# A fused decoder layer: one accumulator per PSUM bank in the first feed-forward product, copies and stores moved from the first to the second block, and a scheduler's cost table rewritten

## The chip, the cores and the metric

The kernel runs on one core of one Trainium2 chip. The metric is the device time of one execution in microseconds (us). Three runs of the kernel before gave 2949.49, 2956.81 and 2946.39 us, median 2949.49. The core's engines each work through a queue of their own in order: PE (TensorE, matrix products into PSUM), DVE (VectorE) and ACT (ScalarE, both elementwise work, both able to read PSUM), POOL (GpSimd) and SP (SyncE, which here only issues the DMAs).

## The reference

One decoder layer on 2048 tokens of width 1024, in fp32. Cut to what matters:

```
proj = x @ w_in                               # q, k, v, z, gates, memory queries
o = gated_delta_rule(conv(q, k, v), gates)    # 8 heads of 128, chunked, a state carried along
m = memory_attention(mq, mem_k, mem_v)        # 4 heads over 256 memory rows
x = layer_norm(ALPHA * x + concat(o, m) @ w_out)
x = layer_norm(ALPHA * x + square(relu(x @ w_ff1)) @ w_ff2)   # width 1024 -> 4096 -> 1024
```

## The kernel before

**Blocks and stages.** The tokens go through in four blocks of 512 (`for b in range(NB)`, near the end of `hybrid_layer`). Each block has a stage with the heads (here MIX: projections, delta rule and memory attention), the output projection (OUT, `out_proj`, with the first layer norm in `norm1`), and the feed-forward part, `ff_seven` (line 1169). That one runs over four groups g of 1024 hidden features. For each group it makes the hidden activations (here FF1) and then their product with `w_ff2` (FF2).

**Precision.** Every fp32 operand is split in two: `hi` is the value rounded to the PE's fp32r (a copy on ACT), `lo` is the remainder (a subtraction on DVE). A product is three matmuls: hi hi, hi lo, lo hi. So a 128x1024 weight tile costs a load, one ACT cast and one DVE subtraction before PE can use it. A tile that was split once can be kept in DRAM as a pair: `keep_hilo` (line 494) stores it, `load_hilo` (line 498) loads both halves with no work on ACT or DVE. `hilo_in` (line 486) loads an fp32 tile and splits it using two of the weight buffers; `hilo(load_raw(...))` (lines 475 and 480) takes three. There are `NW = 11` weight buffers.

**Seven products.** FF2 in all blocks, and FF1 in blocks 1 to 3, use a Winograd form with seven products in place of eight for a 2x2 partition of the operands. The sums of weight parts (`S1`-`S4` of `w_ff1`, `T`-like sums of `w_ff2`) are made in block 0 and kept in DRAM (`fsc`, `tsc`). In FF1 of blocks 1 to 3 the token side is split into `B11, B21, B22, T1-T4` by `to_quads` (line 641) after the layer norm, token groups in the order 2, 3, 0, 1. There a unit v is 256 features; a group has two, so a block has eight. `ff1_quads` (line 1416) runs the seven products of a unit in the order of `FF1_SEVEN` (line 1136). A product is 24 matmuls of 128x256, 12 for each half i of the unit. The accumulators, named A, B and C:

- A gathers A11, S2, S1 and S4 in turn, and is read on the way after each of them. C gathers S3 and A22, and is read after each. B holds A12.
- A and C of one half lie in one PSUM bank, A in the first 256 columns and C in the second. Both halves of B lie in another bank. `read` (line 1444) takes each part out with an ACT copy or a DVE addition, adds the parts up, applies relu and square, and splits the result as input of FF2.
- For the first group both units run interleaved: their A11 and A12 come first, since these need only token groups 2 and 3.

PSUM has eight banks, under five tags: `acc` 3, `ga0`, `ga1` and `m` one each, `pb` 2.

**DRAM traffic around it.** In block 0, FF1 is a plain product. It stores the split parts of every `w_ff1` tile for later (`keep_parts`, line 1144, into `fhl`), and block 0's head iterations issue DRAM-to-DRAM copies of three parts of `w_ff2` (`copy_rows`, line 1114, into `fcp`), which FF2 loads in every block. `load_out` (line 537) splits `w_out` in block 0, stores the pairs (`osc`) and loads them in blocks 1 to 3.

**What sets the order.** Nothing runs when it is written. `Recorder` (line 140) records every operation; `issue` (line 230) then simulates the five engines with a table of durations (`cost`, line 192), latencies between engines (`LAT`, `LAT_FROM`), buffers and one DMA pipe. Each engine takes, of what is ready in that model, the operation with the lowest index (`nc.shift` adds to the index). The resulting order per engine is fixed in the program; at run time semaphores make each engine wait for what it needs.

Of the kernel before, what the change touches and what calls it, by code (L numbers as in the profile page):

```python
# [139 lines left out]
class Recorder:  # L140
# [51 lines left out]
    def cost(o, name, wr, rd, args, kw):  # L192
# [15 lines left out]
        if e == "SP":  # L208
            o.extra = 2100 + _prod(wr[0].shape if wr else rd[0].shape) * 4 / 390.0
            return 450  # L210
        scal = [v for v in args[2:] if isinstance(v, Ref)] if name.startswith("tensor_scalar") else []
        scal += [v for k, v in kw.items() if k in ("scalar", "scalar1", "scale", "bias") and not isinstance(v, (int, float))]
        if e == "ACT":
            n = _prod((wr[0]).shape[1:])
            return 52 + 0.833 * n + (0 if psum else 42) + 93 * len(scal) + ((305 if scal else 198) if "accum_out" in kw else 0)
        if e == "DVE":
            fast = not psum and name in ("tensor_copy", "tensor_scalar_mul", "tensor_scalar_add", "tensor_scalar_max",
                                         "memset")
            return 68 + (0.52 if fast else 1.042) * n + 62 * len(scal) + (7 * n if name == "reciprocal" else 0)
        if name == "memset":  # L220
            return 40 + 0.83 * n
        if kw.get("op") == ALU.pow:
            return 840 + 38 * n
        if name == "tensor_copy":
            return 150 + 1.3 * n
        if name == "tensor_tensor":
            return 150 + 3.5 * n
        return 134 + 3.14 * n if n > 8 else 500 if n == 1 else 200

    def issue(self):  # L230
# [50 lines left out]
        while True:  # L281
# [70 lines left out]
def hybrid_layer(  # L352
# [184 lines left out]
    def load_out(b, u, nh):  # L537
        if b == 0:
            hi, lo = hilo(load_raw(w_out[u, nh]))
            keep_hilo(osc[u, nh], hi, lo)  # L540
        else:
            hi, lo = load_hilo(osc[u, nh])
# [98 lines left out]
    def to_quads(y, Q, keep, t):  # L641
# [11 lines left out]
        if t < 2:  # L653
            nc.shift = 200 if t == 0 else 130
# [12 lines left out]
            quad_split(Q, "T2", t, s["T2"])  # L667
            quad_split(Q, "T3", t, s["T3"])
            quad_split(Q, "B22", t, b22)
            quad_split(Q, "T1", t, s["T1"])  # L670
            quad_split(Q, "T4", t, s["T4"])
# [389 lines left out]
    def mem_attn(h, mq, mkv, cat):  # L1061
# [28 lines left out]
        for m in range(2):  # L1090
# [21 lines left out]
           for g in range(NS) for u in (4 * g, 4 * g + 1) for n in ("B11", "B21", "B22")}  # L1112

    def copy_rows(u):
        nc.after = nc.ops[-1]
        for n in ("B11", "B21", "B22"):
            nc.sync.dma_start(out=fcp[u, n], in_=w_ff2[u + (0 if n == "B11" else 2), 1 if n == "B22" else 0])
        nc.after = None

    def keep_sums(u, j):  # L1120
# [9 lines left out]
        for i, o, x, y in ((1, 0, 1, 0), (3, 1, 3, 1), (2, 3, 3, 0), (4, 2, 2, 3)):  # L1130
# [5 lines left out]
    FF1_SEVEN = (("A11", "B11", "A", False), ("A12", "B21", "B", False), ("S2", "T2", "A", True), ("S3", "T3", "C", False),  # L1136
# [3 lines left out]
    fhl = {(v, n): rec.buf(dr, (P, 2048), F32, "fhl%d_%s" % (v, n), 1, "fhl")  # L1140
           for v in range(2 * NS) for n in ("A11", "A12", "A22", "S1", "S2", "S3", "S4")}
    raws = {}

    def keep_parts(f, hi, lo):
        g, o = f // 8, f % 8
        v, i = 2 * g + (o % 4) // 2, o % 2
        for n, k in (("A11", 0), ("A12", 1)) if o > 3 else (("A22", 1),):
            for h, r in enumerate((hi, lo)):
                c = 1024 * h + 512 * i
                nc.sync.dma_start(out=fhl[v, n][:, c:c + 512].part(h), in_=r[:, 512 * k:512 * (k + 1)].bitcast(F32))  # L1150
# [18 lines left out]
    def ff_seven(b, ff1_tiles, ff1_quads, relu2, add, norm2):  # L1169
# [3 lines left out]
        for g in range(NS):  # L1173
# [29 lines left out]
            for v in range(2):  # L1203
                if b:
                    if v == 0 or g:
                        vs = (0, 1) if g == 0 else (2 * g + v,)
                        acc = {(x, i): bank("af", "pb" if (x, i) == (1, 1) else "acc") for x in vs for i in range(2)}
                        quads = ff1_quads(vs, acc, {x: bank("af", "pb" if g == 0 and x == 1 else "m") for x in vs}, put)
# [4 lines left out]
                for part in ((0, 1, 2, 3),) if g == 0 and v == 0 else ((0,), (1,), (2,), (3,)):  # L1213
# [3 lines left out]
                    for i, a in zip(part, ff1_tiles([fs[i] for i in part], len(part) > 1)):  # L1217
# [20 lines left out]
                        put(v, j, ("S4",), s4[:, 3:4].part(3))  # L1238
            last = g == NS - 1
# [4 lines left out]
            for n, (xn, wn, bn, on, (th, nh)) in enumerate(SEVEN[i] for i in order):  # L1244
# [65 lines left out]
    for b in range(NB):  # L1310
# [16 lines left out]
        for t in range(H + 2):  # L1327
# [11 lines left out]
            elif b == 0 and t <= 2 * NS:  # L1339
                copy_rows(4 * ((t - 1) // 2) + (t - 1) % 2)  # L1340
# [75 lines left out]
        def ff1_quads(vs, ACs, Bs, put):  # L1416

            out = {}

            def step(v, n):  # L1420
                wn, tn, bn, on = FF1_SEVEN[n]
                if wn[0] == "A":
                    hi, lo = load_hilo(fhl[v, wn])
                else:
                    hi, lo = hilo_in(fsc[v, wn])
# [138 lines left out]
```

## Time and profile before

| what | value |
|---|---|
| profiled execution, time | 2947.32 us |
| its span, first to last instruction | 2945.6 us |
| median of three timed runs | 2949.49 us |
| DVE busy | 2289.4 us (78%) |
| ACT busy | 1590.8 us (54%) |
| data moved by DMA | 631.62 MB |
| mean granted clock of PE | 0.991 |

All operations are issued from one line, 335, so instructions are told apart by their tiles. `af<-Thi,wh` is a matmul of FF1 into an accumulator, with `Thi` or `Tx` (tokens) and `wh` or `wl` (weights, hi or lo). `af<-wh,xh` is one of FF2, `ao` one of OUT. `sq<-af` and `sq<-sq,af` are the reads of the FF1 accumulators. `Tx` and `tq` belong to the token-side sums, `pt` to the transposes. In the stretch views the columns are the stretch in us from the span's start, then its length, and for PE, weight loads, DVE, ACT and (where used) POOL the busy us with the number of instructions, then the granted clock, the share of the DMA engines that was busy, and GB/s. Block 0 runs to about 803 us, the others start at 803, 1517 and 2230.

### The profile page before, as it was taken

How to read it: one execution, taken by the hardware profiler on the slowest of the kernel's cores; microseconds unless marked ns; L12 is line 12 of the kernel's file. 1: busy time of each engine (PE TensorE's matmuls, PEld its weight loads, DVE VectorE, ACT ScalarE, POOL GpSimd, SP SyncE). 2: the span in 40 equal slices, each digit the busy share in tenths (PEclk: the TensorE clock that was granted, in tenths of full speed). 3: DMA queues.
4: the chain of work that ended last, by engine and by line, in shares of the span. 5: the costliest groups of instructions: out<-in, count | busy, mean ns of one | idle time of the engine just before them, and what ended most of it. 6: DMA issues, size and time to landing. Idle time of an engine off the chain costs nothing. (4 is left out here: it accounts for less than half of the span.)

```text
span 2945.6 us, 47726 instructions
## 1 busy us (share of the span) xinstructions
PE 2847.1 (97%) x15844; PEld 2427.8 (82%) x15844; DVE 2289.4 (78%) x6128; ACT 1590.8 (54%) x4087; POOL 426.0 (14%) x1051
## 2 busy tenths in 40 slices
PE   8999998999999999999999999999999999999998
PEld 6888777787778888888978888888888888888887
DVE  7999878777888885866688887676668888586668
ACT  6667534544456662655545665255664566355554
POOL 2333200000023320000003331000001332000000
PEclk9999999999999999999999999999999999999999
DMA  7876798988854434566684434556677443456665
GB/s 277 313 258 233 264 346 316 327 300 287 282 207 134 136 122 150 196 227 222 236 286 155 136 122 145 172 193 217 215 264 261 137 136 122 161 172 222 222 217 191
DMA packets 210870, 631.62 MB, mean 214 GB/s; under 512 B 24000, under 2 KB 42816, under 8 KB 210240
## 3 DMA queue, kind: packets, MB, share of 16 engines
q1 hardware_dynamic: 210048, 628.52, 62.2%
q8 instruction: 125, 2.05, 0.3%
q14 instruction: 121, 0.99, 0.1%
q10 hardware_dynamic: 576, 0.06, 0.0%
HBM read 509.93 MB, written 131.14 MB: 218 GB/s over the span
## 5 line engine op out<-in xcount | busy, mean ns | idle before, releaser
L335 ACT CAST wh<-wl 128x1024 fp32r<-128x1024 f32 x320 | 335.2, 1049 | 351.7 <-DMA wl<-fsc 104.4
L335 DVE TENSOR_TENSOR wl<-wl,wh 128x1024 fp32r<-128x1024 f32 x320 | 387.2, 1221 | 139.5 <-ACT wh L335 137.8
L335 PE MATMUL af<-wh,xl 128*128 128x512 f32 x896 | 351.4, 393 | 0.2 <-DVE xl L335 0.2
L335 PE MATMUL af<-Thi,wh 128*128 128x256 f32 (+1 forms) x1056 | 325.5, 309 | 10.0 <-DVE sq L335 5.3
L335 PE MATMUL af<-Thi,wl 128*128 128x256 f32 (+1 forms) x1056 | 324.6, 308 | 10.2 <-DVE wl L335 6.6
L335 PE MATMUL af<-Tlo,wh 128*128 128x256 f32 (+1 forms) x1056 | 325.0, 308 | 6.0 <-DVE sq L335 4.6
L335 PE MATMUL af<-wh,xh 128*128 128x512 f32 x768 | 299.6, 393 | 16.2 <-ACT xh L335 9.2
L335 PE MATMUL af<-wl,xh 128*128 128x512 f32 x768 | 301.9, 393 | 1.4 <-DVE wl L335 1.3
L335 DVE SCALAR_TENSOR_TENSOR y<-y,af 128x512 f32<-128x512 f32 x224 | 151.9, 683 | 106.7 <-PE af L335 106.6
L335 PE MATMUL af<-Tx,wh 128*128 128x256 f32 x1152 | 212.1, 285 | 10.7 <-ACT sq L335 10.5
L335 PEld LDWEIGHTS af<-Thi,wh 128*128 128x128 f32 x1056 | 202.5, 192 | 23.3 <-DVE sq L335 7.1
L335 PEld LDWEIGHTS af<-Thi,wl 128*128 128x128 f32 x1056 | 202.5, 192 | 21.9 <-DVE wl L335 8.3
L335 PEld LDWEIGHTS af<-Tlo,wh 128*128 128x128 f32 x1056 | 202.5, 192 | 17.7 <-DVE sq L335 6.5
L335 PEld LDWEIGHTS af<-wh,xl 128*128 128x128 f32 x896 | 170.0, 190 | 36.2 <-DVE xl L335 0.7
L335 PEld LDWEIGHTS af<-Tx,wh 128*128 128x128 f32 x1152 | 179.5, 192 | 14.2 <-ACT sq L335 13.1
L335 PEld LDWEIGHTS af<-wh,xh 128*128 128x128 f32 x768 | 145.8, 190 | 48.5 <-ACT xh L335 10.3
L335 PEld LDWEIGHTS af<-wl,xh 128*128 128x128 f32 x768 | 145.6, 190 | 32.8 <-DVE wl L335 2.7
L335 PE MATMUL af<-Tx,wl 128*128 128x256 f32 x576 | 163.2, 283 | 0.3
L335 ACT ACTIVATE sq<-sq 128x256 f32<-128x256 f32 x336 | 131.0, 414 | 50.9 <-DVE sq L335 48.8
L335 PE MATMUL ao<-wl,ch 128*128 128x512 f32 x384 | 155.8, 406 | 0.0
L335 PE MATMUL ao<-wh,ch 128*128 128x512 f32 x384 | 152.9, 398 | 1.8 <-ACT wh L335 1.8
L335 PE MATMUL ao<-wh,cl 128*128 128x512 f32 x384 | 153.3, 400 | 0.3 <-DVE cl L335 0.3
(306 smaller groups left out, 7590.6 us busy)
## 6 DMA issues: line engine op xcount, KB each, us to landing
wl<-tsc SPq DMA_DIRECT2D x128, 512.0 KB, 3.4
wh<-wsc SPq DMA_DIRECT2D x108, 512.0 KB, 5.2
wl<-wsc SPq DMA_DIRECT2D x108, 512.0 KB, 4.3
wl<-fcp SPq DMA_DIRECT2D x96, 512.0 KB, 3.5
wl<-fsc SPq DMA_DIRECT2D x96, 512.0 KB, 4.8
wh<-fhl SPq DMA_DIRECT2D x72, 512.0 KB, 3.9
wl<-fhl SPq DMA_DIRECT2D x72, 512.0 KB, 4.1
wsc<-wh SPq DMA_DIRECT2D x36, 512.0 KB, 3.4
```

The source lines that it names most:

```text
L335: o.fn(*[res(a) for a in o.args], **{k: res(v) for k, v in o.kw.items()})
```

## The change

Three things are changed together.

1. **FF1 of blocks 1 to 3.** A of each half gets a bank of its own, of which it uses half. C gets a bank of its own for both halves (`acc`; in the first group `ga0` and `ga1`). B keeps its bank. The order of products is now A12, A11, S3, S2, S1, A22, S4. Reads are recorded after a product's both halves, without column keys, so a read of B or C waits for both halves. A12 isn't read at once but after A11. In the first group three products come ahead of the token sums, not four (A12 and A11 of the first unit, A12 of the second). `to_quads` makes and splits T3 first, then T1 and T2, then T4, with new shifts.
2. **DRAM traffic.** `keep_parts` is gone. For units 0 and 1 `keep_first` loads, splits and stores A11, A12 and A22 in block 0, one tile after each unit of groups 1 to 3. For units 2 to 7 these parts are copied DRAM to DRAM into `fac` and loaded and split in each of blocks 1 to 3 (`hilo_in`). The copies, `fac` and `fcp`, are issued in the head iterations of block 1. FF2 of block 0 reads `w_ff2` itself. `load_out` stores the pairs of `w_out` in block 1 instead of block 0, so block 1 splits them too.
3. **The scheduler's table.** New latencies, durations and a DMA rate of 330 instead of 390 (GB/s in the model); latency within DVE and ACT without the margin; 400 ns before and after SP.

```diff
-LAT = {("PE", "PE"): 0, ("DVE", "DVE"): 130, ("ACT", "ACT"): 155, ("POOL", "POOL"): 100}
-LAT_FROM = {"PE": 200, "DVE": 130, "ACT": 135, "POOL": 75, "SP": 60}
+RATE, FROM_SP, TO_SP = 330.0, 400, 400
+LAT = {("PE", "PE"): 0, ("DVE", "DVE"): 120, ("ACT", "ACT"): 140, ("POOL", "POOL"): 100}
+LAT_FROM = {"PE": 200, "DVE": 130, "ACT": 140, "POOL": 90, "SP": FROM_SP}
+PT3, PT2, PT1, PT4, PT5 = 0, 60, 30, 200, 130
...
-                lat = LAT.get((e, s.eng), LAT_FROM[e])
-                if lat:
-                    lat += MARGIN
+                lat = LAT[e, e] if s.eng == e and e in ("PE", "DVE", "ACT") else LAT_FROM[e] + MARGIN + (TO_SP if s.eng == "SP" else 0)
...
     def load_out(b, u, nh):
-        if b == 0:
-            hi, lo = hilo(load_raw(w_out[u, nh]))
+        if b > 1:
+            return as_rows(*load_hilo(osc[u, nh]))
+        hi, lo = hilo(load_raw(w_out[u, nh]))
+        if b == 1:
             keep_hilo(osc[u, nh], hi, lo)
...
+            nc.shift = PT3 if t == 0 else 0
...
+            sub(s["T3"], b22, s["B12"])
+            quad_split(Q, "T3", t, s["T3"])
+            nc.shift = PT2 if t == 0 else PT1
             sub(s["T1"], b12, keep[t + 2, 0])
             sub(s["T2"], b22, s["T1"])
-            sub(s["T3"], b22, s["B12"])
+            quad_split(Q, "T2", t, s["T2"])
+            nc.shift = PT4 if t == 0 else PT5
             sub(s["T4"], keep[t + 2, 1], s["T2"])
...
+    def keep_first(i):
+        v, n = sorted(fhl)[i]
+        t = unit("wr", dt=F32)
+        col_parts(v, n, t)
+        keep_hilo(fhl[v, n], *hilo(t))
...
+    def copies(v):
         nc.after = nc.ops[-1]
+        u = 4 * (v // 2) + v % 2
         for n in ("B11", "B21", "B22"):
-            nc.sync.dma_start(out=fcp[u, n], in_=w_ff2[u + (0 if n == "B11" else 2), 1 if n == "B22" else 0])
+            nc.sync.dma_start(out=fcp[u, n], in_=row_part(u, n))
+        for n in ("A11", "A12", "A22"):
+            if (v, n) in fac:
+                col_parts(v, n, fac[v, n])
...
-    FF1_SEVEN = (("A11", "B11", "A", False), ("A12", "B21", "B", False), ("S2", "T2", "A", True), ("S3", "T3", "C", False),
+    FF1_SEVEN = (("A12", "B21", "B", False), ("A11", "B11", "A", False), ("S3", "T3", "C", False), ("S2", "T2", "A", True),
                  ("S1", "T1", "A", True), ("A22", "T4", "C", True), ("S4", "B22", "A", True))
...
-                        acc = {(x, i): bank("af", "pb" if (x, i) == (1, 1) else "acc") for x in vs for i in range(2)}
-                        quads = ff1_quads(vs, acc, {x: bank("af", "pb" if g == 0 and x == 1 else "m") for x in vs}, put)
+                        quads = ff1_quads(
+                            vs, {(x, i): bank("af", "pb" if (x, i) == (1, 1) else "acc") for x in vs for i in range(2)},
+                            {x: bank("af", "pb" if g == 0 and x == 1 else "m") for x in vs},
+                            {x: bank("af", "acc" if g else "ga%d" % x) for x in vs}, put)
...
-                        w[v] = as_rows(*hilo_in(tsc[u0 + v, wn] if wn in (1, 2, 3, 4) else fcp[u0 + v, wn]))
+                        w[v] = as_rows(*(
+                            hilo_in(tsc[u0 + v, wn]) if wn in (1, 2, 3, 4) else
+                            hilo_in(fcp[u0 + v, wn]) if b else hilo(load_raw(row_part(u0 + v, wn)))))
...
-            elif b == 0 and t <= 2 * NS:
-                copy_rows(4 * ((t - 1) // 2) + (t - 1) % 2)
+            if b == 1 and 1 <= t <= 2 * NS:
+                copies(t - 1)
...
                 if b == 0:
-                    keep_parts(f, hi, lo)
                     raws[f] = rt
...
+                hi, lo = load_hilo(fhl[v, wn]) if (v, wn) in fhl else hilo_in((fsc if wn[0] == "S" else fac)[v, wn])
                 hi, lo = (r.rearrange("p (a k f) -> p a k f", a=2, k=4) for r in (hi, lo))
                 for i in range(2):
-                    if bn == "B":
-                        o, keys, other = Bs[v][:, 256 * i:256 * i + 256], ("B", i), ("B", 1 - i)
-                        start = i == 0
+                    if bn == "A":
+                        o, start = As[v, i][:, :256], not on
                     else:
-                        o = ACs[v, i][:, 256 * (bn == "C"):256 * (bn == "C") + 256]
-                        keys, other = bn, "C"
-                        start = bn == "A" and not on
+                        o, start = (Bs if bn == "B" else Cs)[v][:, 256 * i:256 * i + 256], i == 0 and not on
...
+                if wn == "A12":
+                    held[v, i] = o
+                    return
...
-                    return
-                q = {"A12": 3, "S1": 0, "A22": 1, "S4": 2}[wn]
+                    if wn != "A11":
+                        return
+                    o = held.pop((v, i))
+                q = {"A11": 3, "S1": 0, "A22": 1, "S4": 2}[wn]
...
-                order.sort(key=lambda x: (x[1] > 1, x[0], x[1]))
+                order.sort(key=lambda x: (x[1] > (x[0] == vs[0]), x[0], x[1]))
```

More of the change, by code (lines that the diff above doesn't have):

```diff
@@ L214, in cost @@
             n = _prod((wr[0]).shape[1:])
-            return 52 + 0.833 * n + (0 if psum else 42) + 93 * len(scal) + ((305 if scal else 198) if "accum_out" in kw else 0)
+            return 52 + 0.833 * n + (0 if psum else 42) + (120 if scal and n < 256 else 93) * len(scal) + ((305 if scal else 225) if "accum_out" in kw else 0)
         if e == "DVE":
-            fast = not psum and name in ("tensor_copy", "tensor_scalar_mul", "tensor_scalar_add", "tensor_scalar_max",
+            fast = not psum and n > 200 and name in ("tensor_copy", "tensor_scalar_mul", "tensor_scalar_add", "tensor_scalar_max",
                                          "memset")
@@ L220, in cost @@
         if name == "memset":
[L221 removed]
+            return 105 + 0.83 * n
         if kw.get("op") == ALU.pow:
[L223 removed]
+            return 700 + 105 * n
         if name == "tensor_copy":
[L225 removed]
+            return 250 + n
         if name == "tensor_tensor":
[L227 to L228 removed]
+            return 245 + 3.5 * n
+        return 80 + 4.2 * n if n > 8 else 660 if n == 1 else 280
     def issue(self):
@@ L1112, in hybrid_layer, with col_parts, row_part @@
            for g in range(NS) for u in (4 * g, 4 * g + 1) for n in ("B11", "B21", "B22")}
-    def copy_rows(u):
+    fac = {(v, n): rec.buf(dr, (P, 1024), F32, "fac%d_%s" % (v, n), 1, "fac")
+           for v in range(2, 2 * NS) for n in ("A11", "A12", "A22")}
+    fhl = {(v, n): rec.buf(dr, (P, 2048), F32, "fhl%d_%s" % (v, n), 1, "fhl")
+           for v in range(2) for n in ("A11", "A12", "A22")}
+    def col_parts(v, n, t):
+        f = 8 * (v // 2) + 2 * (v % 2) + 4 * (n != "A22")
+        c = slice(0, 512) if n == "A11" else slice(512, 1024)
+        nc.sync.dma_start(out=t.rearrange("p (f c) -> p f c", f=2), in_=w_ff1[f:f + 2, :, c].rearrange("f p c -> p f c"))
+    def keep_first(i):
[3 more added lines that the diff above has]
+        keep_hilo(fhl[v, n], *hilo(t))
+    def row_part(u, n):
+        return w_ff2[u + (0 if n == "B11" else 2), 1 if n == "B22" else 0]
+    def copies(v):
         nc.after = nc.ops[-1]
+        u = 4 * (v // 2) + v % 2
         for n in ("B11", "B21", "B22"):
-            nc.sync.dma_start(out=fcp[u, n], in_=w_ff2[u + (0 if n == "B11" else 2), 1 if n == "B22" else 0])
+            nc.sync.dma_start(out=fcp[u, n], in_=row_part(u, n))
+        for n in ("A11", "A12", "A22"):
+            if (v, n) in fac:
+                col_parts(v, n, fac[v, n])
         nc.after = None
@@ L1139, in hybrid_layer @@
            for v in range(2 * NS) for n in ("S1", "S2", "S3", "S4")}
-    fhl = {(v, n): rec.buf(dr, (P, 2048), F32, "fhl%d_%s" % (v, n), 1, "fhl")
-           for v in range(2 * NS) for n in ("A11", "A12", "A22", "S1", "S2", "S3", "S4")}
     raws = {}
[L1144 to L1150, printed above, removed]
     def ff1_sums(f):
@@ L1238, in ff_seven @@
                         put(v, j, ("S4",), s4[:, 3:4].part(3))
+                if b == 0 and g:
+                    keep_first(2 * g - 2 + v)
             last = g == NS - 1
@@ L1438, in step @@
                         for m, (a, x) in enumerate(((hi, th), (hi, tl), (lo, th))):
-                            first = start and k == 0 and m == 0
-                            nc.tensor.matmul(o.part(keys, other) if first else o.part(keys), a[:, i, k], x, start=first,
+                            nc.tensor.matmul(o, a[:, i, k], x, start=start and k == 0 and m == 0,
                                              stop=k == 3 and m == 2, skip_group_check=True)
-                    reads.append((v, n, i, o.part(keys)))
+                    reads.append((v, n, i, o))
             def read(v, n, i, o):
                 wn = FF1_SEVEN[n][0]
+                if wn == "A12":
+                    held[v, i] = o
+                    return
                 if (v, i) not in out:
@@ L1477, in ff1_quads @@
             if len(vs) > 1:
-                order.sort(key=lambda x: (x[1] > 1, x[0], x[1]))
+                order.sort(key=lambda x: (x[1] > (x[0] == vs[0]), x[0], x[1]))
             reads = []
             for v, n in order:
-                if n > 1:
-                    for q in [q for q in reads if q[0] == v]:
-                        read(*q)
-                    reads[:] = [q for q in reads if q[0] != v]
                 step(v, n)
-                if n > 1 or v == vs[0]:
-                    for q in [q for q in reads if q[0] == v]:
-                        read(*q)
-                    reads[:] = [q for q in reads if q[0] != v]
+                for q in reads:
+                    read(*q)
+                reads.clear()
                 if n == 6:
```

21 lines of the change are left out of this document (6 added, 15 removed).

## The prediction

> **What bounds the kernel now.** I read the page first, then the list of PE's waits, then the busy time by stretch.
>
> ```profile
> span 2945.6 us, 47726 instructions
> PE 2847.1 (97%) x15844; PEld 2427.8 (82%) x15844; DVE 2289.4 (78%) x6128; ACT 1590.8 (54%) x4087; POOL 426.0 (14%) x1051
> ```
> ```profile
> PE af L335 <- DVE sq L335: 13.0, 24, 0.6
> PE af L335 <- ACT sq L335: 11.8, 16, 1.8
> PE af L335 <- ACT xh L335: 9.2, 3, 3.9
> PE af L335 <- DVE wl L335: 7.9, 8, 1.3
> PE aq L335 <- ACT Thi L335: 7.4, 1, 7.4
> PE af L335 <- ACT wh L335: 7.0, 2, 6.0
> PE af L335 <- DVE tq L335: 4.4, 3, 1.7
> ```
> ```profile
> 7.00:803.00 796.00, 759.06 (x3741) 625.28 (x3742) 659.90 (x1681) 426.39 (x990) 118.86 (x263) 0.97 0.83 293
> 803.00:1517.00 714.00, 697.84 (x4043) 601.57 (x4042) 540.83 (x1482) 389.01 (x1035) 103.80 (x262) 1.00 0.56 188
> ```
> ```profile
> 328.00:436.00 108.00, 98.39 (x475) 78.10 (x474) 85.59 (x225) 36.78 (x105) 11.77 (x26) 0.95 0.91 320
> 488.00:535.00 47.00, 40.36 (x167) 32.12 (x167) 37.05 (x54) 20.64 (x24) 0.00 (x0) 0.93 0.92 338
> 535.00:579.00 44.00, 44.00 (x196) 36.45 (x195) 32.08 (x66) 22.15 (x36) 0.00 (x0) 1.00 1.01 351
> ```
> ```profile
> 803.00:1094.00 291.00, 287.34 (x1566) 239.70 (x1565) 244.72 (x975) 170.76 (x593) 89.17 (x230) 1.00 0.45 149
> 1094.00:1180.00 86.00, 85.33 (x427) 69.65 (x427) 50.56 (x112) 23.59 (x76) 9.38 (x20) 1.00 0.47 161
> 1269.00:1312.00 43.00, 41.45 (x338) 40.56 (x337) 26.95 (x47) 30.84 (x65) 0.00 (x0) 1.00 0.68 227
> ```
>
> PE is the bound: it idles 2945.6 - 2847.1 = 98.5 us. The change leaves the number of matmuls as it is, so its gain is cut out of those 98.5 us and of whatever a lowered clock costs. Of the idle time 37 us (796 - 759) lie in block 0 and 16 in block 1. Block 0 has the DMA engines 83% busy, block 1 56%, and its granted clock is 0.97 against 1.00. In blocks 1 to 3 the largest idle items are the first two waits of the list, for reads of FF1's accumulators.
>
> **Term 1: reads of the FF1 accumulators.** What such a wait is:
>
> ```profile
> 1192.48 0.28 PE L335 MATMUL af<-Thi,wh 128*128 128x256 f32 x1
> 1192.60 0.28 PE L335 MATMUL af<-Tlo,wh 128*128 128x256 f32 x1
> 1193.39 0.39 PE L335 MATMUL af<-Thi,wl 128*128 128x256 f32 x1 [0.52 <-DVE sq L335]
> ```
> ```profile
> 1192.01 0.68 DVE L335 TENSOR_TENSOR Tlo<-pt,Thi 128x512 fp32r<-128x512 f32 x1
> 1192.91 0.42 DVE L335 TENSOR_TENSOR sq<-sq,af 128x256 f32<-128x256 f32 x1 [0.22 <-PE af L335]
> ```
>
> Matmuls start every 0.12 us. After the one at 1192.60 the next comes at 1193.39; in between DVE reads. The `hi lo` matmul at 1192.60 is not the last of its half (a half ends with `lo hi`), so DVE isn't reading what PE is about to add to. It reads another part of the bank, waits for the running matmul to leave the bank, and PE waits for it. Start to start 0.79 where 0.12 is due: 0.67 lost, 0.15 more than the 0.52 listed. Over the list: 24 + 16 = 40 waits, 13.0 + 11.8 = 24.8 us, and 40 x 0.15 = 6, so 31 us in blocks 1 to 3. With A in a bank per half and B and C read when both halves stand, no read falls beside a write to its bank: upper bound -31.
>
> What comes in their place: S1 now follows S2 into the same A. Half 0's S2 must be copied out in the 12 matmuls of half 1, 1.44 us.
>
> ```profile
> L335 ACT COPY sq<-af 128x256 f32<-128x256 f32 x144 | 52.7, 368 | 43.5 <-PE af L335 42.1
> L335 ACT CAST wh<-wl 128x1024 fp32r<-128x1024 f32 x320 | 335.2, 1049 | 351.7 <-DMA wl<-fsc 104.4
> L335 DVE TENSOR_TENSOR wl<-wl,wh 128x1024 fp32r<-128x1024 f32 x320 | 387.2, 1221 | 139.5 <-ACT wh L335 137.8
> ```
>
> The matmul's end (0.28) and the copy (0.37) take 0.65; some 0.7 us are left. If ACT has just begun a cast (1.05), PE waits up to 0.3, with all FF1 matmuls queued behind. There are 24 units x 2 halves = 48 such places; even if half of them wait 0.25, that is 6 us. So I take -31 + 6 = **-25** (bounds -31 and 0). C's and B's reads have at least one whole product, 2.88 us, before the next write.
>
> **Term 2: the start of the first group.** The waits for `tq` (4.4) and part of `wl` sit here.
>
> ```profile
> 1188.40 0.28 PE L335 MATMUL af<-Thi,wl 128*128 128x256 f32 x1
> 1190.22 0.39 PE L335 MATMUL af<-Thi,wh 128*128 128x256 f32 x1 [1.54 <-DVE tq L335]
> ```
>
> The wait at 1190.22 is for bank `m`: B of the first unit takes it after the transposes of token group 1, when the T1 subtraction has read them. That stays so. T3 first makes the first sum ready earlier by some subtractions, but one product less is ahead of it, and C now takes `ga0`, whose transposed rows are read last by the split of B22, the end of the list. If S3 keeps its place before S2 on PE, it waits for about six DVE operations of 0.68 us (the 512-column row above, itself such a split), 4 us a block; if S2 passes it, nothing. I take **0**, bounds -4 and +12.
>
> **Term 3: block 0's feed-forward part.** Its stretches show FF1 at a DMA share of 1.01 (351 GB/s), then FF2 with PE waiting.
>
> ```profile
> ACT wh L335 <- DMA wl<-tsc: 29.4, 20, 3.8
> ```
> ```profile
> PE af L335 <- DVE wl L335: 4.0, 5, 1.0
> ```
> ```profile
> 569.81 1.12 SPq L335 DMA_DIRECT2D fhl<-wh  x2
> ...
> 571.91 1.06 SPq L335 DMA_DIRECT2D fhl<-wl  x2
> ...
> 574.20 0.39 SPq L335 DMA_DIRECT2D wl<-tsc  x1
> ```
> ```profile
> 668.57 0.39 PE L335 MATMUL af<-wh,xl 128*128 128x512 f32 x1
> 671.11 0.50 PE L335 MATMUL af<-wh,xh 128*128 128x512 f32 x1 [2.15 <-ACT xh L335]
> ...
> 672.69 0.63 PE L335 MATMUL af<-wh,xh 128*128 128x512 f32 x1
> ...
> 674.40 0.63 PE L335 MATMUL af<-wl,xh 128*128 128x512 f32 x1
> ```
>
> The first row is of ACT, the second of PE, both from the feed-forward part of block 0 alone. The FF2 weights (`tsc`) are issued behind the stores of kept parts and land late. ACT stands at a cast for them, and relu and the split (`xh`) stand behind it in ACT's queue. Cost to PE: `xh` 9.2, `wh` 7.0, `wl` 4.0, 20 us. Then the clock: after the wait that ends at 671.11 the five matmuls from 672.69 to 674.40 come 0.43 us apart, where twice 0.12 is due for twice the columns; seven of them lose 1.3 us. Four waits in the list can be that long (three of `xh`, the 6.0 of `wh`): 5 us more. Together 25.
>
> A rule of the Trainium skill bears on this: TensorE: Matmul & The Clock Gate, section "What's actually happening", lets the clock drop to half after an idle window of about 3.4 us. Here a wait of 2.15 us is followed by doubled spacing, so the measurement is harsher than the rule; by the rule only the two longest waits (6.0 and 3.9) would have a slow tail, and the 5 us would be 2.6.
>
> ```profile
> fcp<-in_w_ff_dram SPq DMA_DIRECT2D x24, 512.0 KB, 7.1
> fhl<-wh SPq DMA_DIRECT2D x48, 256.0 KB, 3.2
> osc<-wh SPq DMA_DIRECT2D x12, 512.0 KB, 4.8
> ```
>
> Removed are 96 stores (48 hi, as many lo) of 0.26 MB, 6.3 MB and 24 issues for each of four groups; `keep_first` puts back two tiles of 1.5 MB in groups 1 to 3. The stretch 535 to 579 moves 351 x 44 = 15.4 MB; with 12.2 the share is 0.80. The raw `w_ff2` loads take a third weight buffer, and an SP load that waits for a buffer holds all loads behind it; that is why I take two thirds of the 25, **-17** (bounds -25 and 0).
>
> **Term 4: block 0's output projection.** PE idles 108 - 98.4 = 9.6 us there at a clock of 0.95 and a DMA share of 0.91; block 1's stretch idles 0.7 at 0.47. The 24 stores of `w_out` pairs (12.6 MB of the 34.6 that 320 GB/s move in 108 us) leave it, the 12.6 MB of copies leave the stage ahead of it. **-6** (bounds -13 and 0).
>
> **Term 5: block 1 takes them over.** 42 copies of 0.52 MB are 22 MB, 63 us at 351 GB/s: 0.45 + 63/291 = 0.67 of DMA time in MIX. OUT: 12.6 MB stored, 6.3 less read, 18 us: 0.47 + 18/86 = 0.68. Block 0 did its own at 0.83 and lost. **+3** (bounds 0 and +10, what terms 4 and 5 have in block 0).
>
> **Term 6: more splits.** Six parts in each of three groups and three blocks, 54, and 12 for `w_out` in block 1, 6 for `keep_first`: 72 x (1.05 + 1.22) us on ACT and DVE. They lie beside matmuls: in FF1 of a later group ACT is busy 30.84 of 43 us, with 6 casts more 37; DVE goes from 27 to 34. **+3** (bounds 0 and +57, all 54 casts on the path).
>
> **Term 7: the table.** It reorders everything. In MIX and OUT of block 1 PE idles 3.7 and 0.7 us, so little can be won there, and a fixed order that misjudges one chain costs a few us: **+2** (bounds -4 and +12).
>
> Sum: -25 + 0 - 17 - 6 + 3 + 3 + 2 = **-40**. The profiled execution took 2947.3 us (span and 1.7 us around it), which makes 2907; the median of the runs is 2.2 us higher. I write 2908.
>
> **The rivals.**
>
> - *The reads still stop PE.* C and B still hold two halves in one bank, and the S2-S1 turn is tighter. Against it: the wait shown was for another part of the bank. Term 1 is 0: 2907 + 25 = 2932.
> - *The loss moves with the stores.* Block 1 then loses what block 0 lost: terms 3 and 4 come back, 2930. Against it: block 1 starts from 0.45, not from 0.83.
> - *Banks run short.* A unit now takes all three `acc` banks, so the next unit's A and C wait for the last reads of this one. At nine hand-overs (g = 1 to 3, three blocks), three banks each, 0.67 us: +18, 2925. For: all eight banks are taken. Against: A12 runs first on `m`, 2.88 us. The Trainium skill, PSUM — Partial Sum Buffer, section "Summary: rules for kernel authors", says to evacuate promptly; holding A12 goes against that rule.
> - *ACT becomes the bound in FF1* (slower). If the 12 us that ACT idles in 43 are waits in its chain and can't be filled, every added cast lengthens FF1: 54 x 1.05 = 57 in place of 3, 2961. It decides from about 40 us, three quarters of the casts on the path. Against: casts of a product can run during FF2 as far as buffers go.
> - *Terms 1 and 3 both fail:* 2907 + 25 + 17 = 2949, no change.
>
> **How the numbers follow.** About 0.3%, 9 us, can be told from no change. Chances: forecast 0.53; banks 0.05; reads 0.13; moved loss 0.13; these four are faster, 0.84. Both fail 0.08: same. ACT 0.08: slower. The range reaches up to the two rivals at 2930 and 2932 with 10 us of unknown costs, 2942, and down to the bounds of terms 1, 3 and 4 (-69): 2878.
>
> **What would show it.** Right: PE's waits for `sq` fall from 24.8 us to under 8; the share of 1.01 goes to about 0.8; block 0 idles 15 to 20 us in place of 37; 72 more casts with no longer FF1 stretches. Wrong: waits for `sq` as before; new waits of `ao` or MIX matmuls in block 1; ACT over 40 of 43 us in FF1; stretches of blocks 1 to 3 that don't shorten by about 8 us each.

## The result, and the profile after

The changed kernel takes 2870.55 us (median of 4 runs, 2869.47 to 2871.62), the kernel before beside it 2951.59 (4 runs, 2946.39 to 2956.81). The ratio is 0.9725, with a 95% interval of 0.9706 to 0.9744: 81 us faster, where 40 were forecast. The time lies 7 us under the low end of the predicted range. The profiled execution took 2871.62 us.

The page of the changed kernel (busy us, share and instructions of each engine; then the casts of weights with count, busy, mean ns, idle before them):

```profile
span 2869.8 us, 47642 instructions
PE 2819.9 (98%) x15844; PEld 2426.1 (85%) x15844; DVE 2358.7 (82%) x6200; ACT 1658.2 (58%) x4159; POOL 417.3 (15%) x1051
...
L335 ACT CAST wh<-wl 128x1024 fp32r<-128x1024 f32 x350 | 366.0, 1047 | 261.8 <-DMA wl<-fcp 70.5
```

PE runs the same 15844 matmuls. Its idle time went from 98.5 to 49.9 us, a gain of 48.6. But its *busy* time fell too, from 2847.1 to 2819.9. Two things lie in those 27.2 us. PE was busy for 36.1 us at a granted clock of 0.5 before and for 21.1 us after; with matmuls taking twice as long there (0.43 us apart in place of 0.23), some 7.5 us of the fall are the clock, an estimate. The rest fits waits: the modelled tail of a matmul covers the first part of a wait behind it, so that of the 0.67 us lost at 1193.39 only 0.52 are listed. The 98.5 us out of which, beside the clock, the prediction cut its gain were therefore too small a store.

The stretches of the changed kernel: the four blocks; then block 0's OUT, late FF1 and FF2; then MIX and OUT of block 1 and the FF1 stretch of a later group:

```profile
8.00:771.00 763.00, 747.69 (x3742) 623.41 (x3743) 664.83 (x1694) 434.05 (x996) 116.27 (x263) 0.99 0.73 252
771.00:1470.00 699.00, 692.32 (x4042) 601.22 (x4041) 572.15 (x1506) 417.14 (x1064) 100.12 (x262) 1.00 0.66 218
```
```profile
330.00:425.00 95.00, 92.48 (x464) 75.52 (x463) 82.86 (x218) 36.70 (x98) 10.64 (x25) 0.98 0.65 214
473.00:517.00 44.00, 41.47 (x173) 32.83 (x172) 36.13 (x52) 18.97 (x22) 0.00 (x0) 0.96 0.89 314
517.00:560.00 43.00, 43.00 (x191) 35.63 (x190) 33.78 (x68) 24.10 (x38) 0.00 (x0) 1.00 0.93 300
```
```profile
771.00:1056.00 285.00, 284.97 (x1577) 241.41 (x1576) 246.50 (x952) 176.25 (x603) 84.26 (x231) 1.00 0.66 218
1056.00:1143.00 87.00, 84.67 (x416) 69.02 (x414) 60.96 (x141) 30.37 (x77) 10.28 (x19) 1.00 0.76 264
1229.00:1269.00 40.00, 40.00 (x336) 40.00 (x335) 30.01 (x48) 32.33 (x67) 0.00 (x0) 1.00 0.58 184
```

Block 0 is 33 us shorter: its idle time goes from 37 to 15, its clock from 0.97 to 0.99. Block 1's MIX now carries the copies (DMA share 0.66, 0.67 expected) and still got shorter, 291 to 285. The FF1 stretch went from 43 to 40 us, with ACT at 32.33 of 40.

PE's longest waits in the changed kernel, and further down the list what is left of the waits for `sq`:

```profile
PE af L335 <- DVE wl L335: 9.8, 8, 2.6
PE aq L335 <- ACT Thi L335: 8.0, 1, 8.0
PE pt L335 <- issue: 2.5, 1, 2.5
PE af L335 <- DVE tq L335: 2.1, 3, 0.7
...
PE af L335 <- ACT sq L335: 1.3, 3, 0.4
```

The waits for `sq` fell from 24.8 us (40) to 1.3 (3), those for `xh` are gone.

To compare kernels by stage I cut each trace at the first matmul of every stage, which is told by the operands (`aq`, `ao`, `af` with T, `af` with x). This is arithmetic on start times, so it also counts what hides in "busy". The last stage ends with the last matmul, so a column adds up to less than its span. Each column is one profiled execution; that of the DRAM part alone was the fastest of ten runs, 6 us under their median, so its column is too good by that much. Times in us:

```
                before   FF1 only  DRAM only  table only  changed
block 0         795.8    798.2     778.4      788.0       762.9
  MIX           320.5                                     321.8
  OUT           107.8    109.2     104.0      106.9        94.9
  FF1           183.7    181.3     180.8      179.6       179.0
  FF2           183.8    185.9     176.1      181.3       167.3
blocks 1-3 MIX  866.3    863.7     859.3      857.4       856.4
           OUT  258.5    258.4     262.1      251.9       253.8
           FF1  540.3    508.9     550.3      539.8       506.5
           FF2  466.1    468.0     466.1      474.2       470.8
span           2945.6   2916.2    2936.2     2930.2      2869.8
```

Two stages hold most of the gain: block 0 (-32.9) and FF1 of blocks 1 to 3 (-33.8). MIX gives -9.9, OUT -4.7, FF2 takes +4.7.

### The profile page after: what moved, and what is told of

Read it like the earlier page. It is cut to its first block, busy times and chain, and to the rows that moved or that the text cites. A ratio compares the mean times of both kernels' runs of the same rounds, so it can differ in the third digit from the quotient of the medians.

```text
span 2869.8 us, 47642 instructions
## 1 busy us (share of the span) xinstructions
PE 2819.9 (98%) x15844; PEld 2426.1 (85%) x15844; DVE 2358.7 (82%) x6200; ACT 1658.2 (58%) x4159; POOL 417.3 (15%) x1051
## 5 line engine op out<-in xcount | busy, mean ns | idle before, releaser
L335 ACT CAST wh<-wl 128x1024 fp32r<-128x1024 f32 x350 | 366.0, 1047 | 261.8 <-DMA wl<-fcp 70.5
L335 DVE TENSOR_TENSOR wl<-wl,wh 128x1024 fp32r<-128x1024 f32 x350 | 420.3, 1218 | 70.3 <-ACT wh L335 70.2
L335 PE MATMUL af<-wh,xh 128*128 128x512 f32 x768 | 292.5, 390 | 1.4 <-ACT wh L335 1.4
L335 ACT CAST wh<-wr 128x1024 fp32r<-128x1024 f32 (+1 forms) x132 | 136.6, 1041 | 116.8 <-DMA wr<-in_w_ff_dram 53.6
L335 DVE TENSOR_TENSOR wl<-wr,wh 128x1024 fp32r<-128x1024 f32 (+1 forms) x132 | 158.5, 1203 | 22.5 <-ACT wh L335 12.5
```

The lines of the kernel that those rows point to most:

```text
L335: o.fn(*[res(a) for a in o.args], **{k: res(v) for k, v in o.kw.items()})
```

## The experiments: the three parts, alone and left out

The theory S was that the parts add up and that the table's share is the difference, found mostly in the later blocks. First each part alone on the kernel before.

**FF1 part alone** (item 1 of the change on the kernel before, nothing else).

> Only the FF1 part of the change: banks, product order, token sums; the old table and the old DRAM traffic. Theory S (each part acts in its own stage): the FF1 stretches of blocks 1 to 3 shorten by 34 us together as in the changed kernel, nothing else moves, so about -34 us (2915). Rival R (the rewritten table makes the order fit, and with the old one the new turns of S1 after S2 wait): -15 us or less, with PE waits for sq of 10 us or more. My prediction's terms 1 and 2: -25.

**DRAM part alone** (item 2).

> Only the DRAM part: kept parts, copies and stores moved; the old FF1 and the old table. Theory S: block 0 shortens by 33 us as in the changed kernel, blocks 1 to 3 lose about 5 to the additional splits, so -28 us (2922). Rival R (block 0's stalls come from an order made with a DMA rate that is too high, and the traffic matters less): -12 us or less. My prediction's terms 3 to 6: -17.

**Table alone** (item 3).

> Only the scheduler's table. Theory S: the head stage and the output projection of blocks 1 to 3 shorten by 15 us together, block 0's feed-forward part stays, so -15 us (2935). Rival R: block 0's feed-forward waits shrink with the same traffic, since loads are placed earlier: -30 us or more, of which 15 in block 0. My prediction's term 7: +2.

Then the changed kernel less one part: without the table, without the DRAM part, without the FF1 part.

> The change with the old table: FF1 part and DRAM part together. Theory S: the parts add up, -62 us (2888), and the table is worth the missing 15 to 20. Rival R: clearly less than the sum of the two parts alone, -45 us or less, with waits back in block 0 and at the turn from S2 to S1. By my prediction, with the table at +2, it would be as fast as the changed kernel.

> The FF1 part and the table, with the old DRAM traffic. Theory S2 (the FF1 part acts by itself, 31 us; DRAM traffic and table need one another in block 0, where the old traffic keeps the DMA engines full): block 0 as with the table alone, about 788 us against 763 in the changed kernel; in all -48 us (2898). Rival R2 (the table needs the new FF1, not the new traffic): -65 us or more, block 0 under 775.

> The DRAM part and the table, with the old FF1. Theory S2: block 0 takes about 763 us as in the changed kernel, and the FF1 stretches of blocks 1 to 3 stay near 545, since the added splits make the shared banks costlier; in all -42 us (2904). Rival R2: block 0 stays over 775, and in all -30 us or less.

Measured, ratios to the kernel before with their 95% intervals; us are the ratio's distance from 1 times 2947:

```
part    alone: ratio              us    all but it: ratio         us    its worth on top
FF1     0.9894 [0.9879, 0.9910]  -31    0.9814 [0.9792, 0.9837]  -55    -26
DRAM    0.9991 [0.9981, 1.0000]   -3    0.9873 [0.9854, 0.9893]  -37    -44
table   0.9938 [0.9921, 0.9955]  -18    0.9838 [0.9823, 0.9853]  -48    -33
```

S was right for FF1 (-34 expected) and nearly for the table (-15), and wrong for the DRAM part: -28 expected, -3 measured. The singles add up to 52, the whole is 81. Of the kernels less one part none took the time that its theory gave: without the table -48 (S: -62, its rival: -45 or less), without the DRAM part -37 (-48 expected), without the FF1 part -55 (-42 expected). So the parts help one another, and the stages say where.

- *FF1 and DRAM.* DRAM alone takes 17 us off block 0 and gives back 10 in FF1 of blocks 1 to 3 (540.3 to 550.3), where PE's waits for `sq` rise. With the FF1 part the same additional splits cost nothing there: without the table FF1 is 505.1, against 508.9 for FF1 alone. The list of PE's waits with DRAM alone:

```profile
PE af L335 <- DVE sq L335: 17.6, 33, 0.6
PE af L335 <- ACT sq L335: 12.2, 18, 1.8
```

- *DRAM and table.* Block 0 is 778.4 and 788.0 us with one of them, 763.6 with both (without the FF1 part): 32 where the singles make 25. With both, FF1 is 524.3 us even in the old banks, not the 545 expected, and its waits for `sq` are 16.3 us:

```profile
PE af L334 <- ACT sq L334: 8.6, 9, 2.1
PE af L334 <- DVE sq L334: 7.7, 15, 0.5
```

- *FF1 and table without DRAM* get in each other's way: -37 where the singles make -49. Block 0 is 788.3 as expected, but FF2 of blocks 1 to 3 is 481.8 us, 16 more than before.

A second timing of the changed kernel, as a control beside one of the kernels below, gave 2871.98 us, ratio 0.9745 [0.9723, 0.9767]. By that ratio each worth on top is 6 us smaller (the table's 27, not 33), which changes no reading:

> The changed kernel once more, beside these three on the same chip, so that single digits can be compared: 2868 to 2874.

## The experiments: block 0

What PE waits for in block 0's feed-forward part, in four kernels. DRAM part alone:

```profile
PE af L335 <- ACT xh L335: 8.2, 3, 3.3
PE af L335 <- DVE wl L335: 1.5, 2, 0.8
PE af L335 <- ACT wh L335: 1.2, 1, 1.2
```

Table alone:

```profile
PE af L334 <- DVE wl L334: 10.6, 9, 2.7
PE af L334 <- ACT wh L334: 6.2, 3, 3.9
```

The changed kernel:

```profile
PE af L335 <- DVE wl L335: 3.6, 3, 2.6
PE af L335 <- ACT wh L335: 1.4, 1, 1.4
```

Before, there were 20.2 us: `xh` 9.2, `wh` 7.0, `wl` 4.0. With the traffic gone the weights come on time and the waits for `wh` and `wl` shrink from 11.0 to 2.7, but `xh` stays at 8.2. With the table alone `xh` is gone and the weights' waits grow to 16.8. Only both leave 5.0. Why `xh` survives is read from ACT's queue. ACT's wait for the FF2 weights, DRAM part alone and then changed:

```profile
ACT wh L335 <- DMA wl<-tsc: 24.5, 20, 3.0
```
```profile
ACT wh L335 <- DMA wl<-tsc: 9.2, 10, 2.2
```

In the old order ACT stands in 20 places at a cast whose weights are still on the way, and relu and `xh` stand behind it. A scheduler whose model lets a load land too early would put the casts there. Four kernels test which entries of the table matter.

**Changed kernel with the old DMA model.**

```diff
-RATE, FROM_SP, TO_SP = 330.0, 400, 400
+RATE, FROM_SP, TO_SP = 390.0, 60, 0
...
-            return 400
+            return 450
```

> The changed kernel with the old model of DMAs alone: rate 390, issue 450 ns, 60 ns after a DMA and nothing ahead of one. Theory S2 (the order gives loads too little time, so casts stand on ACT for weights that are late): most of the table's 33 us comes back, 2890 or more, with block 0's FF2 over 175 us. Rival (it is the latencies and durations of the engines): under 2878.

2882.29 us, 0.9783 [0.9764, 0.9803]: about 12 us over the changed kernel, between both expectations. In the profiled execution the loss lies in block 0 (775.8 against 762.9): 9 us in FF1 and FF2, 6 in OUT, while MIX is 2 shorter. In the feed-forward part the old picture is back, ACT's wait and then PE's:

```profile
ACT wh L335 <- DMA wl<-tsc: 25.1, 20, 2.7
```
```profile
PE af L335 <- ACT xh L335: 7.4, 3, 3.5
```

**Changed kernel with the old latencies** (`LAT`, `LAT_FROM` and the margin as before).

> The changed kernel with the old latencies between engines and within them, margin included; DMA model and durations as changed. Theory S2: 2870 to 2880, the head stages of blocks 1 to 3 together up to 5 us longer. Rival (the latencies carry the table's gain): 2890 or more.

2873.45 us, 0.9754 [0.9735, 0.9773], in all as the theory said; nothing that these runs can tell from the changed kernel. By stage it is not as expected: MIX of blocks 1 to 3 gets 5.7 us shorter, not longer (850.7 against 856.4), and OUT 9.1 longer (262.9 against 253.8); in block 0 OUT is 9.4 longer (104.3 against 94.9) and FF2 8.0 shorter (159.3 against 167.3). The border between MIX and OUT shifts with the order, so the two are best read together.

**Changed kernel with the old durations** (the bodies of `cost` for ACT, DVE and POOL as before).

> The changed kernel with the old durations of operations on ACT, DVE and POOL; DMA model and latencies as changed. With the old DMA model the changed kernel lost 12 us, with the old latencies little; the old table as a whole costs 33. Theory S2a (the parts of the table add up): the durations are worth the remaining 15 us, 2885, most of it in the head stages. Rival (no single group carries it, they stand in for one another): 2876 or less.

2873.44 us, 0.9750 [0.9730, 0.9771]: the same, which is the rival's result. By stage the durations do two opposite things: with the old ones block 0 takes 752.9 us (762.9 and 760.9 in two executions of the changed kernel) and MIX of blocks 1 to 3 takes 865.6 (856.4 and 858.9).

So no single group of entries carries the table's worth on top: left out one at a time they cost 12, 3 and 3 us by the medians, not about 30. The last test puts the DMA model alone on the kernel before.

```diff
-LAT_FROM = {"PE": 200, "DVE": 130, "ACT": 135, "POOL": 75, "SP": 60}
+LAT_FROM = {"PE": 200, "DVE": 130, "ACT": 135, "POOL": 75, "SP": 400}
...
-            o.extra = 2100 + _prod(wr[0].shape if wr else rd[0].shape) * 4 / 390.0
-            return 450
+            o.extra = 2100 + _prod(wr[0].shape if wr else rd[0].shape) * 4 / 330.0
+            return 400
...
-                    lat += MARGIN
+                    lat += MARGIN + (400 if s.eng == "SP" else 0)
```

> The kernel before with the new DMA model alone: rate 330, issue 400 ns, 400 ns after a DMA and ahead of one. Theory S3 (in block 0 it is the model of the DMAs that keeps casts off ACT's queue until their weights are there, and it needs the lighter traffic): block 0 shortens by under 10 us, in all -10 us, 2936. Rival (the model is enough by itself): block 0 by 15 or more, PE's waits for xh gone, -20 us or more.

2929.41 us, 0.9939 [0.9915, 0.9962]: -18, as much as the whole table alone (10 expected; 20 or more by the rival). Block 0 falls by 7.9, FF1 of blocks 1 to 3 by 9.5. PE's waits in block 0's feed-forward part:

```profile
PE af L335 <- ACT wh L335: 9.8, 3, 4.7
PE af L335 <- DVE wl L335: 9.3, 8, 2.9
```

No `xh`, and the late weights now stop PE itself. The DMA entries alone bring about this change of the order. They gain nothing by it there: the waits are 19.1 us in place of 20.2, and FF1 and FF2 of block 0 take 366.8 us together where they took 367.5 (360.9 with the whole table alone). Block 0's gain lies in MIX and OUT, 7.3 us together, and OUT alone falls from 107.8 to 95.8 us with its DMA share still at 0.92, no traffic having moved:

```profile
333.20:429.00 95.80, 92.30 (x468) 74.23 (x467) 77.19 (x202) 34.89 (x96) 9.33 (x19) 1.00 0.92 326
```

## The experiments: FF1 of blocks 1 to 3

The FF1 part does several things at once: whole reads, a bank of its own for A, a new order of products. Theory B: a read that falls beside a write to its bank stops PE, wherever it happens. It expects a loss both from reading by half (two halves of B or C in one bank) and from A and C sharing a bank. The other theories hold that one of the two, or the order, does it.

In the trace such a stop is a wait for a semaphore. In the prediction's example the read at 1192.91 waits for the semaphore of the matmul at 1192.60, and the weight load for the matmul at 1193.39 waits for that of the read. The scheduler's log (`Recorder`, `add`) tells the parts of a bank apart by keys, so its simulation has PE wait for no such read, while the built program does. What the chip would do without the semaphores no run here shows.

With the FF1 part alone the waits for `sq` are already gone:

```profile
PE af L336 <- ACT sq L336: 0.6, 4, 0.2
```

**Changed kernel, reads by half.** Each half of B and C is read when it stands, while PE writes the other half of the bank; A12 is copied out first, as before the change.

```diff
+                        keys, both = ((bn, i),), ((bn, 0), (bn, 1))
...
-                    reads.append((v, n, i, o))
+                    reads.append((v, n, i, o.part(*keys)))
...
-                if wn in ("A11", "S2", "S3"):
+                if wn in ("A12", "S2", "S3"):
```

> The changed kernel, but the products into B and C are read half by half as each half stands, and A12 is copied out first, A11 added; the same number of reads, matmuls and banks. Theory B (a read beside a write to another half of the same bank stops PE): PE waits for sq come back, two thirds of the 31 us or about 20, 2890, in the FF1 stretches. Rival O (the order of the products gives the gain, the banks don't matter): within 5 us of the changed kernel.

2909.92 us, 0.9875 [0.9854, 0.9896]: 38 us lost, more than B expected. FF1 is 549.3 us. The waits, and one of them on PE's timeline (start, length, operation, wait before it):

```profile
PE af L335 <- ACT sq L335: 17.6, 36, 0.8
PE af L335 <- DVE sq L335: 13.3, 27, 0.5
```
```profile
1235.31 0.28 PE L335 MATMUL af<-Thi,wl 128*128 128x256 f32 x1
1236.05 0.39 PE L335 MATMUL af<-Thi,wh 128*128 128x256 f32 x1 [0.46 <-ACT sq L335]
```

0.74 us from start to start where 0.12 is due, as in the kernel before.

**Changed kernel, A and C of a half in one bank again,** whole reads kept.

```diff
-                        o, start = (Bs if bn == "B" else Cs)[v][:, 256 * i:256 * i + 256], i == 0 and not on
+                        o, start, keys = As[v, i][:, 256:], False, ("C",)
```

> The changed kernel, but A and C of one half share a bank again, as before; order of products, whole reads and all else as changed. Theory B: reads of C fall beside S2's and S4's writes to A and reads of A beside writes to C, so 25 us or more come back in the FF1 stretches, 2895 or more. Rival O: within 5 us of the changed kernel. Rival P (the third acc bank that a unit takes costs something): below 2868.

2865.63 us, 0.9725 [0.9700, 0.9750], with the changed kernel beside it at 0.9745: not slower. B fell in this form. Rival P (a unit's third bank costs something) named a time below 2868 and got it, with FF2 of blocks 1 to 3 at 466.6 us against 471.2, but the intervals of the two kernels overlap. What is left of PE's waits for `sq`:

```profile
PE af L335 <- DVE sq L335: 1.5, 3, 0.5
```

The reason is the order of the halves. A product runs half 0 and then half 1, each half in a bank of its own. When half 0 is read, PE writes half 1's bank. Sharing hurts only if the read comes later than 12 matmuls, 1.44 us. That can be made to happen:

**Changed kernel, reads by half, but each half of B in a bank of its own and C beside A.**

```diff
+                    elif bn == "B":
+                        o, start = Bs[v, i][:, :256], True
+                        keys = both = ("B",)
...
+                        o, start, keys = As[v, i][:, 256:], False, ("C",)
```

> The changed kernel with products into B and C read half by half, and the two halves of B in two banks; A and C of a half share a bank. No read falls while the other half of its bank is written. Theory B (the bank decides): as fast as the changed kernel, 2865 to 2878, PE waits for sq under 6 us. Rival H (reading half by half as such stops PE): 2900 or more, as with B and C halves in one bank.

2882.28 us, 0.9776 [0.9749, 0.9803], between the two expectations; 28 of the 38 us came back. What is left, on DVE and then on PE:

```profile
1257.90 1.22 DVE L335 TENSOR_TENSOR wl<-wl,wh 128x1024 fp32r<-128x1024 f32 x1
1259.03 0.42 DVE L335 TENSOR_TENSOR xl<-sq,xh 128x256 fp32r<-128x256 f32 x1
1259.37 0.41 DVE L335 TENSOR_TENSOR ss<-sq,ss 128x256 f32<-128x256 f32 x1
1260.04 0.75 DVE L335 TENSOR_TENSOR sq<-sq,af 128x256 f32<-128x256 f32 x2 [0.26 <-PE af L335]
```
```profile
1259.72 0.28 PE L335 MATMUL af<-Thi,wh 128*128 128x256 f32 x1
1260.52 0.39 PE L335 MATMUL af<-Tlo,wh 128*128 128x256 f32 x1 [0.51 <-DVE sq L335]
```

DVE was busy with a split of 1.22 us and two short operations, so its read of A came late, beside a write to C in the same bank. PE has 18 waits for reads by DVE left, 9.1 us (under 6 expected by B); nine stand at this place of a unit.

**Kernel before, B read when whole** (one line), the edit the other way round.

```diff
-                    reads.append((v, n, i, o.part(keys)))
+                    reads.append((v, n, i, o.part(("B", 0), ("B", 1)) if bn == "B" else o.part(keys)))
```

> The kernel before with one thing changed: a read of B waits for both its halves. Theory B: the 24 PE waits on DVE's sq (13.0 us, with restarts 16) go, -16 us, 2930, in the FF1 stretches of blocks 1 to 3. Rival O (it is the order of the products): under 5 us.

2939.51 us, 0.9965 [0.9951, 0.9979]: -10 (16 expected). In the profiled execution only 5.1 us of that lie in FF1 of blocks 1 to 3 (540.3 to 535.2), at the limit of the rival's 5; block 0, which the edit touches only through the order, is 5.4 shorter. Of PE's 24 waits for reads by DVE, which were all to go, 12 went; those for ACT stayed:

```profile
PE af L335 <- ACT sq L335: 13.3, 16, 1.8
PE af L335 <- DVE sq L335: 7.2, 12, 1.5
```

The 12 that went were reads of B. The 12 that stay all stand in the second half of a unit's last product: PE adds S4 to A, and DVE reads A22 from C late, in the same bank. So A and C in one bank did cost something in the old kernel. One of them, PE and then DVE:

```profile
1306.02 0.28 PE L335 MATMUL af<-Thi,wh 128*128 128x256 f32 x1
1306.81 0.38 PE L335 MATMUL af<-Tlo,wh 128*128 128x256 f32 x1 [0.51 <-DVE sq L335]
```
```profile
1306.33 0.42 DVE L335 TENSOR_TENSOR sq<-sq,af 128x256 f32<-128x256 f32 x1 [0.58 <-PE af L335]
```

**What theory B doesn't cover.** In the kernel before, 10 of the 40 waits, with 9.1 of the 24.8 us, end at the first matmul of a half, which adds to the accumulator that the read takes out. One of them, the first matmul of S2 after ACT's copy of A11:

```profile
1296.20 0.36 ACT L335 COPY sq<-af 128x256 f32<-128x256 f32 x1
1296.62 0.50 PE L335 MATMUL af<-Tx,wh 128*128 128x256 f32 x2 [0.41 <-ACT sq L335]
```

ACT comes to that copy late, straight from casts, and S2 must wait for it in any bank. By start times these ten waits lose 10.7 us and the other thirty 20.4. With the new order of products the ten are gone even where halves are read singly (2909.92 us: of its waits for `sq`, none that the list counts is of this kind), so about a third of what FF1 gained is owed not to the banks but to the new order of products or what came with it. Which of these does it was not isolated.

**A and C in one bank, with the old latencies as well,** a try at a version better than the changed kernel.

> The changed kernel with A and C of a half in one bank and the old latencies. If both add up: block 0 as with the old latencies (FF2 near 159 us) and FF2 of the later blocks as with the shared bank, 2858. If an order is only redrawn each time: 2862 to 2876.

2870.86 us, 0.9739 [0.9715, 0.9762]. The gains don't add. No version tried was faster than the changed kernel beyond the intervals; the shared bank alone, 2865.63 against 2871.98 in the same comparison, comes nearest, and 6 us with overlapping intervals settle nothing.

## Why the prediction was wrong in size

The direction was right and the time was 7 us under the range. Against the profiled execution (2871.6 for 2907 by the sum) 36 us are missing. By its own terms:

- **Term 7, the table (+2, bounds -4 and +12): the step that failed.** Measured -18 alone and -27 to -33 on top of the rest. The working asked only what PE idles in MIX and OUT of block 1, 3.7 and 0.7 us, and found nothing to win. Two things were wrong in that. The listed idle time is no bound: with the table alone these two stages became 4.5 and 2.7 us shorter. And the table was given no effect in block 0, where it is worth most on top of the rest: 783.9 us without it, 762.9 with it. There its DMA entries decide how often a cast stands in ACT's queue for weights that are still on the way (20 places and 25.1 us with the old entries, 10 and 9.2 with the new).
- **Terms 3 and 4 (-17 and -6): mis-sized, with half the cause missing.** Measured -21.2 (FF1 -4.7, FF2 -16.5) and -12.9 in OUT, both inside their bounds. Moving the traffic alone gave -10.6 and -3.8. The prediction saw that `xh` stands behind a late cast, and put the whole wait down to the lateness; the other half is the order, and `xh` stayed at 8.2 us until the table changed that. The clock was charged too little: PE was busy for 18.3 us at a granted clock of 0.5 in block 0's feed-forward part before and for 6.8 after, which an estimate makes 9 us before, where the sum had 5, and 3 after. For OUT the traffic is not shown to be the cause: with the DMA model alone it took 95.8 us at a share of 0.92. MIX and OUT of block 0 together gained 6.8 us by the traffic alone, 7.3 by that model alone and 11.6 in the changed kernel.
- **Term 1 (-25, bounds -31 and 0): right in mechanism for two thirds, too small.** Alone -31.4 in FF1 of blocks 1 to 3, -33.8 in the changed kernel, past the bound. The 6 us taken off for the turn from S2 to S1 did not come: all waits for `sq` together are 1.3 us. The working put all 40 waits down to reads of another part of the bank. That holds for thirty, 20.4 us; the other ten, 10.7 us, wait for A itself, and that they went too is luck as far as this reasoning goes. Of the reason given, "a bank per half for A" turned out not to be needed; whole reads of B and C, and halves that alternate between banks, are what counts.
- **Term 2 (0):** the waits for `tq` went from 4.4 to 2.1 us; right within its bounds.
- **Term 5 (+3):** too high. With the traffic alone block 1's OUT became 3.0 us longer (86.2 to 89.2), but its MIX 5.7 shorter (290.6 to 284.9); in the changed kernel OUT is 0.5 longer (86.7) and MIX 5.3 shorter.
- **Term 6 (+3):** the casts rose by 72 as counted. With the old banks FF1 became 10 us longer by the DRAM part, with the FF1 part not at all. FF2 of blocks 1 to 3 rose by 4.7, but not by the splits: it stayed at 466.1 us with the DRAM part alone and rose to 474.6 with the DMA model alone.
- **The rivals.** "The reads still stop PE" and "the loss moves" did not happen: 1.3 us of waits for `sq`, and block 1 shorter with 0.66 of DMA time in MIX. "ACT becomes the bound" neither: 32.33 of 40 us, where about 40 of 43 was named as the limit. "Banks run short" did not happen, although A12 is held and all banks are taken. The Trainium skill, PSUM — Partial Sum Buffer, section "Summary: rules for kernel authors", would have A12 evacuated promptly; here the trace shows no loss from holding it, with 1.3 us of waits for `sq`. Holding alone was not tested: the two kernels that copy A12 out first, 2909.92 and 2882.28 us, also read by half.

The predicted signs held as far as they went: waits for `sq` under 8, block 0's idle time 15 us, 72 more casts with no longer FF1 stretches. One missed: late FF1 of block 0 still has a DMA share of 0.93, where about 0.8 was expected. It moves 300 x 43 = 12.9 MB (12.2 expected), and a byte took more of the DMA engines' time than before (0.93 at 300 GB/s, 1.01 at 351).

What stays open. Which entries of the table move what besides the DMA model: durations and latencies can be left old one at a time at no cost that can be measured, and all entries together are worth 27 to 33 us. They stand in for one another, but how was not traced. Why MIX of blocks 1 to 3 gained in every one-part kernel (2.6 to 8.9 us) was not isolated. And in FF1 the order of the scheduler and the whole reads share a part of the gain: traffic and table in the old banks already bring 540.3 down to 524.3.

## What to carry to other kernels

Judge what there is to win on an in-order engine by the spacing of its instructions' starts against the nominal spacing, not by listed idle time: the tail of a pipelined matmul hides the beginning of each wait. When the order is fixed by a cost model, a transfer that the model lands too early puts its consumer at the head of a queue in front of work that is ready, so moving the traffic and correcting the model must be valued together, not one by one. Before giving accumulators more banks, look at which writes run while one is read; reading a bank only when nothing more is written to it may cost one line.

## What was not expected of the hardware

- Keeping a read by ACT or DVE apart from writes to another part of the same bank, as the program's semaphores do, costs PE 0.74 to 0.80 us from one matmul's start to the next (1235.31 to 1236.05, 1259.72 to 1260.52), where 0.12 is due, and the profile lists only 0.46 to 0.51 of it as a wait.
- PE's busy time fell by 27.2 us with the number of matmuls unchanged. The Trainium skill warns of the measure (Perfetto Trace Analysis, section "Identifying the Most-Contended Engine": matmul busy share is no good measure of how close a kernel is to its limit; weight-load share is one of the two that it names instead), and the trace agrees: weight loads stayed at 2427.8 and 2426.1 us while the span fell by 75.8.
- 54 more casts and splits on ACT and DVE in blocks 1 to 3 left no trace in FF1's time once PE no longer stopped for reads: 505.1 us with them and 508.9 without (changed kernel without the table, and FF1 part alone, one execution each).
